# The ten weight buffers of a mixer and MoE layer moved to multiples of 256 bytes in SBUF

## Chip, cores and metric

One Trainium2 chip, one of its cores. The metric is the device time of one execution in microseconds (us), the median of several runs. The profile is one further execution with the hardware profiler on; its times are given from the start of its span, which is the time between the first and the last instruction.

## The reference

One layer on 256 tokens of width 1024, all float32. A layer norm comes first. Then two attentions run side by side from one projection `h @ w_in` (1024 x 5120): a differential attention with 4 heads and a chunk attention with 8. Their outputs go through a projection each, are gated, added, and go through `w_out`; a second norm follows. The mixture of experts takes most of the weights:

```python
logits = (t @ w_router + b_router)                  # 32 experts
top_val, top_idx = lax.top_k(logits, TOP_K)         # the best 4 of them for each token
...
hb = xb @ w_exp_in[e] + b_exp_in[e]                 # 1024 -> 2 x 1024
g = jnp.minimum(hb[:, :D_FF], SWIGLU_LIMIT)
u = jnp.clip(hb[:, D_FF:], -SWIGLU_LIMIT, SWIGLU_LIMIT)
a = g * jax.nn.sigmoid(SWIGLU_ALPHA * g) * (u + 1.0)
return a @ w_exp_out[e] + b_exp_out[e]              # 1024 -> 1024
...
h = layer_norm(DEEPNORM_ALPHA * h + f, ln2_g, ln2_b)
```

Each expert has 8 MiB of `w_exp_in` and 4 MiB of `w_exp_out`, so the 32 of them are 384 MiB that must be read once.

## The kernel before

The first part (up to some 200 us) does the norm, the projection, both attentions, the merge and `w_out`. Weights of this part are split on the chip into two float32r parts, which three matmuls multiply (L169 to L171). After it comes the router, and then a loop over 32 places (`for pos in range(NE)`, L1286). Each place takes one expert: its tokens are gathered with one-hot matmuls (L1094), `gemm1` multiplies them with `w_exp_in` (L1144 for 64 token rows, L1147 for 32), `act` is the SwiGLU, `gemm2` multiplies with `w_exp_out` (L1200), and `scatter` adds the gated result to four PSUM banks (L1214). A last norm and the stores end the kernel.

**Buffers of weights.** All large weights land in buffers of 16,384 bytes in each of the 128 partitions, 2 MiB each. There are ten, in four pools: ring_a has five, ring_b two, ring_d one and ring_c two. The loads of `w_in` (13 parts), the branch weights and `w_out` use ring_a alone. From the experts on, a transfer takes the next buffer of a written order, round and round:

```python
order = (ring_b,) * 2 + (ring_a,) * 3 + (ring_d,) + (ring_a,) * 2 + (ring_c,) * 2
```

Each expert is six transfers: four of `w_exp_in` (`load_in`, L983), each of whose descriptors carries 16 KB of one partition, and two of `w_exp_out` (`load_out`, L995), whose descriptors carry 8 KB (the last of them is cut in two). So 192 buffers are filled, by 193 transfers, and after five experts the 30 places of three rounds begin anew. SP issues them all, in the order of the program; a buffer is free again when the matmuls that read it are done. Rows of `w_in` are 2 KB in the buffer.

**Pools.** A partition's memory is filled from both ends. From the left stand const, ring_a, keep, mid, ring_b and ring_d; from the right late, heads and early, which are closed in turn, and ring_c takes late's place. A tile takes its size rounded up to 32 bytes. By the allocation of the kernel before, in bytes of a partition:

| pool | begins at | behind a multiple of 256 | buffers |
|---|---|---|---|
| ring_a | 31,520 | 32 | 5 |
| ring_b | 147,200 | 0 | 2 |
| ring_d | 179,968 | 0 | 1 |
| ring_c | 196,576 | 224 | 2 |

ring_c ends at 229,344, the end of what the right side begins with.

`sub08` and `nlam`, which the change joins, are one column each: DVE writes sub08 at L351 and nlam in `small_1` (L371), and DVE reads them in `differences` (L560) and `finish_a` (L596).

Of the kernel before, what the change touches and what calls it, by code (L numbers as in the profile page):

```python
# [9 lines left out]
F32 = mybir.dt.float32  # L10
# [10 lines left out]
P = 128  # L21
# [23 lines left out]
def kernel(  # L45
# [19 lines left out]
    const = ctx.enter_context(tc.tile_pool(name="const", bufs=1))  # L65
# [2 lines left out]
    es_late, es_heads, es_early = ExitStack(), ExitStack(), ExitStack()  # L68

    keep = ctx.enter_context(tc.tile_pool(name="keep", bufs=1))  # L70
    late = es_late.enter_context(tc.tile_pool(name="late", bufs=1, side="right"))
    heads = es_heads.enter_context(tc.tile_pool(name="heads", bufs=1, side="right"))
    early = es_early.enter_context(tc.tile_pool(name="early", bufs=1, side="right"))
# [266 lines left out]


    bg = const.tile([P, 16], F32, name="bg")
    sub08 = const.tile([P, 1], F32, name="sub08")
    nlam = const.tile([P, 1], F32, name="nlam")
    g1p = early.tile([P, 2 * KC], F32, name="g1p")
    wrg = const.tile([P, KC, NE], F32, name="wrg", tag="wrg")
    rows = const.tile([P, 2, NE], F32, name="rows")
# [338 lines left out]
    def load_rows(src, rows, name, ring):  # L686

        w = wslot(ring, name).rearrange("p (k c) -> p k c", k=4)
        nc.sync.dma_start(w, src[rows:rows + 512, :].rearrange("(k p) c -> p k c", p=P))
        return w  # L690

    wba = load_rows(w_branch_a[0], 0, "wba", ring_a)
    wbb = load_rows(w_branch_b[0], 0, "wbb", ring_a)
    mid = ctx.enter_context(tc.tile_pool(name="mid", bufs=1))
    ring_b = ctx.enter_context(tc.tile_pool(name="ring_b", bufs=2))
    wo = [load_rows(w_out[0], i * 512, f"wo{i}", ring_a) for i in range(2)]

# [711 lines left out]
```

## Time and profile before

| | |
|---|---|
| runs | 1134.95, 1135.90 and 1136.48 us, median 1135.9 |
| profiled execution | 1135.54 us, of which 1133.8 are its span |
| mean granted TensorE clock | 0.947 of full speed |
| busy share of the span | PE 84%, weight load 37%, DVE 25%, ACT 17%, POOL 4% |
| moved by DMA | 438.58 MB, 387 GB/s on the mean |
| chain of work that ended last | DMA 62%, PE 30%, DVE 2%, ACT 1% |

PE is TensorE's matmuls; its busy time is an average over stages with different limits, and so is the DMA rate. The chain is followed back from the last instruction, at each step to what released it. Where it names a DMA, the piece reaches from the issue of the transfer to its landing.

### The profile page before, as it was taken

The page shows a single profiled execution, that of the slowest core. Times are in us where ns is not written, and L with a number is a line of the kernel's source. Part 1 is how long each engine was busy: PE and PEld are TensorE (multiplying, and loading weights), DVE is VectorE, ACT ScalarE, POOL GpSimd, SP SyncE. Part 2 cuts the span into 40 slices and gives each one's busy share as a digit, 9 for nine tenths or more (in the row PEclk, how much of TensorE's full clock was granted, in tenths as well). Part 3 has the DMA queues.
Part 4 walks back from the last instruction along what each step waited for, and adds up shares of the span by engine and source line. Part 5 has one row for each costly group of instructions (what it writes and reads, how often), then busy time and mean ns, then how long its engine had stood idle before and what let it go on. Part 6 is the DMA issues. An engine that isn't in the chain of part 4 may idle for free.

```text
span 1133.8 us, 14138 instructions
## 1 busy us (share of the span) xinstructions
PE 951.6 (84%) x5771; PEld 424.3 (37%) x5771; DVE 282.8 (25%) x640; ACT 191.4 (17%) x412; POOL 48.2 (4%) x77
## 2 busy tenths in 40 slices
PE   8999999999999877878897968787878787878764
PEld 7999998433333222222232312122222122222211
DVE  7687577421111111111111111111111011011113
ACT  4366653211010000000000000000000000000010
POOL 3201200100010000000000000000000000000001
PEclk9999999999999999999898989899989898999978
DMA  8943568899999999999999999999999999999994
GB/s 289 384 174 136 201 249 351 326 403 426 425 412 426 429 426 428 427 425 429 426 425 425 427 428 426 427 425 428 427 425 426 424 428 427 427 427 427 427 423 182
DMA packets 52442, 438.58 MB, mean 387 GB/s; under 512 B 5070, under 2 KB 5422, under 8 KB 19858
## 3 DMA queue, kind: packets, MB, share of 16 engines
q1 hardware_dynamic: 50818, 433.90, 92.0%
q0 software_dynamic: 1120, 3.05, 0.8%
q8 instruction: 47, 0.77, 0.3%
q10 hardware_dynamic: 432, 0.66, 0.2%
q14 instruction: 25, 0.20, 0.1%
HBM read 436.14 MB, written 1.45 MB: 386 GB/s over the span
## 4 chain that ended last, share of the span: by engine, by line
DMA 62%; PE 30%; DVE 2%; ACT 1%; issue 1%; DVEq 0%; SPq 0%; ACTq 0%
DMA w<-in_w_exp_in_dram 52%; DMA w<-in_w_exp_out_dram 10%; PE gu L1144 7%; PE py L1200 4%; PE gu L1147 3%; PE pT L169 2%; PE pT L170 2%; PE pT L171 2%; PE acc L1214 2%; PE px L1094 1%; PE br L171 1%; PE br L170 1%; PE br L169 1%; PE mo L169 1%; PE mo L171 1%; PE mo L170 1%
## 5 line engine op out<-in xcount | busy, mean ns | idle before, releaser
L1144 PE MATMUL gu<-w,xe 128*64 128x512 f32 x1024 | 238.3, 614 | 55.2 <-DMA w<-in_w_exp_in_dram 55.0
L1147 PE MATMUL gu<-w,xe 128*32 128x512 f32 x1024 | 150.5, 720 | 87.5 <-DMA w<-in_w_exp_in_dram 87.5
L1200 PE MATMUL py<-w,aTe 128*64 128x512 f32 (+1 forms) x1024 | 174.8, 604 | 8.6 <-DMA w<-in_w_exp_out_dram 5.4
L1144 PEld LDWEIGHTS gu<-w,xe 128*64 128x64 f32 x1024 | 74.9, 140 | 209.2 <-issue 147.3
L1172 DVE TENSOR_SCALAR a<-gu 128x512 f32<-128x512 f32 (+1 forms) x32 | 17.9, 558 | 468.1 <-PE gu L1144 249.9
L1173 ACT ACTIVATE sg<-a 128x512 f32<-128x512 f32 (+1 forms) x32 | 16.7, 523 | 524.2 <-DVE a L1172 524.2
L1147 PEld LDWEIGHTS gu<-w,xe 128*32 128x32 f32 x1024 | 31.1, 120 | 186.7 <-DMA w<-in_w_exp_in_dram 132.1
L1200 PEld LDWEIGHTS py<-w,aTe 128*64 128x64 f32 (+1 forms) x1024 | 49.9, 124 | 110.3 <-issue 89.4
L169 PE MATMUL pT<-hT_hi,w 128*128 128x256 f32 x256 | 74.0, 289 | 0.0
L170 PE MATMUL pT<-hT_lo,w 128*128 128x256 f32 x256 | 72.4, 283 | 0.0
L171 PE MATMUL pT<-hT_hi,w 128*128 128x256 f32 x256 | 72.4, 283 | 0.0
L1207 DVE COPY y<-py 128x256 f32<-128x256 f32 x32 | 13.6, 425 | 218.1 <-ACT y L1206 212.9
L1214 PE MATMUL acc<-y,st 64*128 64x512 f32 x248 | 61.6, 615 | 0.0
L164 DVE TENSOR_TENSOR w<-win,w 128x512 fp32r<-128x512 f32 (+1 forms) x70 | 51.2, 757 | 31.6 <-ACT w L163 31.6
L163 ACT CAST w<-win 128x512 fp32r<-128x512 f32 (+1 forms) x74 | 46.2, 654 | 33.4 <-PE pT L170 23.1
L1094 PE MATMUL px<-h,oh 128*32 128x256 f32 (+1 forms) x392 | 49.5, 465 | 0.7 <-ACT xe L1119 0.7
L169 PEld LDWEIGHTS pT<-hT_hi,w 128*128 128x128 f32 x256 | 49.0, 191 | 2.2 <-issue 1.4
L170 PEld LDWEIGHTS pT<-hT_lo,w 128*128 128x128 f32 x256 | 49.1, 192 | 0.0
L171 PEld LDWEIGHTS pT<-hT_hi,w 128*128 128x128 f32 x256 | 49.0, 192 | 0.0
L119 POOL TENSOR_TENSOR ln_r<-ln_ve,nhalf 128x1 f32<-128x1 f32 x6 | 3.4, 560 | 849.0 <-DVE ln_ve L117 848.0
L1206 ACT COPY y<-py 128x256 f32<-128x256 f32 x32 | 11.9, 373 | 156.5 <-PE py L1200 156.5
L1214 PEld LDWEIGHTS acc<-y,st 64*128 64x128 f32 x248 | 21.3, 186 | 33.9 <-issue 19.2
(329 smaller groups left out, 827.6 us busy)
## 6 DMA issues: line engine op xcount, KB each, us to landing
w<-in_w_exp_in_dram SPq DMA_DIRECT2D x128, 2048.0 KB, 39.1
w<-in_w_exp_out_dram SPq DMA_DIRECT2D x63, 2048.0 KB, 39.1
win<-in_w_in_dram SPq DMA_DIRECT2D x9, 2048.0 KB, 17.8
wo<-in_w_out_dram SPq DMA_DIRECT2D x2, 2048.0 KB, 7.8
win<-in_w_in_dram SPq DMA_DIRECT2D x4, 512.0 KB
wba<-in_w_branch_a_dram SPq DMA_DIRECT2D x1, 2048.0 KB
wbb<-in_w_branch_b_dram SPq DMA_DIRECT2D x1, 2048.0 KB
w<-in_w_exp_out_dram SPq DMA_DIRECT2D x2, 1024.0 KB, 38.3
```

The source lines that it names most:

```text
L163: A.copy(hi, part)
L164: (eng[k // step % len(eng)] if isinstance(eng, tuple) else eng).tensor_tensor(lo, part, hi, op=ALU.subtract)
L169: T.matmul(dst, a[0], b[0], start=first, stop=False)
L170: T.matmul(dst, a[0], b[1], start=False, stop=False)
L171: return T.matmul(dst, a[1], b[0], start=False, stop=last)
L1094: T.matmul(px[i * w:(i + 1) * w, :], oh[:, t, :], h1[:, t, i * n:(i + 1) * n], start=(t == 0), stop=(t == NT - 1))
L1144: T.matmul(gu[i][q * w:(q + 1) * w, :], lhsT, rows[:, i, q * c:(q + 1) * c], start=first, stop=last)
L1147: T.matmul(both[q * w:(q + 1) * w], lhsT, rows[:, :, q * c:(q + 1) * c], start=first, stop=last)
L1172: V.tensor_scalar(g, gu[0], SW_LIMIT, None, op0=ALU.min)
L1173: A.activation(sg, g, AF.Sigmoid, scale=SW_ALPHA)
L1200: T.matmul(py[r:r + w, :], lhsT, w2[i][:, q, j, n * 512:(n + 1) * 512], start=(i == 0 and (m == 0 or w < CAP and m < 2)), stop=(i == 1 and ...
L1214: T.matmul(acc[t][n], st[r, t, :], y[r, :], start=False, stop=False)
```

## The change

A pool edge of 56 floats (224 bytes) is put at the right end, ahead of late, heads and early; the two tiles of one column in const become two columns of one tile, which makes const 32 bytes shorter; and a tile of 8 floats (32 bytes) is put at the start of mid. Nothing uses edge and mid_pad. By that the right side moves down by 224 bytes, ring_c to 196,352, which is 767 x 256 and just where ring_d ends; ring_a and keep move down by 32, ring_a to 31,488, which is 123 x 256; ring_b (575 x 256) and ring_d (703 x 256) stay where they are. No instruction is added, taken away or moved.

```diff
@@ -68,6 +68,9 @@
     keep = ctx.enter_context(tc.tile_pool(name="keep", bufs=1))
+
+    edge = ctx.enter_context(tc.tile_pool(name="edge", bufs=1, side="right"))
+    edge.tile([P, 56], F32, name="edge")
     late = es_late.enter_context(tc.tile_pool(name="late", bufs=1, side="right"))
@@ -340,8 +343,8 @@
     bg = const.tile([P, 16], F32, name="bg")
-    sub08 = const.tile([P, 1], F32, name="sub08")
-    nlam = const.tile([P, 1], F32, name="nlam")
+    two_cols = const.tile([P, 2], F32, name="two_cols")
+    sub08, nlam = two_cols[:, 0:1], two_cols[:, 1:2]
     g1p = early.tile([P, 2 * KC], F32, name="g1p")
@@ -692,6 +695,7 @@
     mid = ctx.enter_context(tc.tile_pool(name="mid", bufs=1))
+    mid.tile([P, 8], F32, name="mid_pad")
     ring_b = ctx.enter_context(tc.tile_pool(name="ring_b", bufs=2))
```

## Rows read from the trace of the kernel before

**Rows 1.** The page's slices, 40 of 28.3 us each: the busy share of the 16 DMA engines in tenths, and what they moved.

```profile
DMA  8943568899999999999999999999999999999994
GB/s 289 384 174 136 201 249 351 326 403 426 425 412 426 429 426 428 427 425 429 426 425 425 427 428 426 427 425 428 427 425 426 424 428 427 427 427 427 427 423 182
```

**Rows 2.** The table by stage, for the part with the experts: the stretch, its length, the busy time of PE, weight load, DVE, ACT and POOL (with counts of instructions), the granted clock, the DMA share and GB/s.

```profile
255.00:366.00 111.00, 107.37 (x692) 36.77 (x694) 19.00 (x52) 12.46 (x28) 6.53 (x17) 1.00 1.01 423
366.00:500.00 134.00, 108.01 (x636) 33.94 (x628) 18.62 (x50) 11.58 (x25) 0.00 (x0) 0.95 1.01 427
500.00:700.00 200.00, 159.60 (x864) 50.37 (x864) 26.84 (x69) 14.88 (x32) 0.00 (x0) 0.93 1.01 426
700.00:900.00 200.00, 155.51 (x866) 48.16 (x862) 25.12 (x67) 15.16 (x33) 0.00 (x0) 0.93 1.01 427
900.00:1100.00 200.00, 153.75 (x866) 47.83 (x870) 26.16 (x68) 15.87 (x36) 0.00 (x0) 0.91 1.01 427
```

**Rows 3.** The chain that ended last, in order of time: start, length, what. Between the third and the fourth row stand 15 more pieces of weights of 39 to 41 us, with short pieces of PE between them.

```profile
358.36 7.11 PE py L1200 x32
365.49 32.52 DMA w<-in_w_exp_in_dram
403.10 39.73 DMA w<-in_w_exp_in_dram
...
1068.84 40.95 DMA w<-in_w_exp_in_dram
1109.83 3.22 PE gu L1147 x16
```

**Rows 4.** What SP waited for before its issues from 366 to 1100 us: us in total, times, longest; and the page's issues of expert weights: count, size, median us from issue to landing.

```profile
SPq L983 <- DMA w<-in_w_exp_out_dram: 101.7, 48, 3.5
SPq L995 <- DMA w<-in_w_exp_in_dram: 98.9, 49, 3.4
SPq L983 <- DMA w<-in_w_exp_in_dram: 82.3, 48, 3.1
SPq L983 <- PE py L1200: 44.4, 25, 3.2
...
w<-in_w_exp_in_dram SPq DMA_DIRECT2D x128, 2048.0 KB, 39.1
```

**Rows 5.** The DMA engines' busy share in tenths from 180 to 260 us, 40 slices of 2 us.

```profile
DMA  9999999046999981089999999998799999999999
```

**Rows 6.** SP's issues in order of time: start, time until the last of them is out, line, transfer and count.

```profile
580.19 17.62 SPq L983 DMA_DIRECT2D w<-in_w_exp_in_dram  x4
...
609.71 19.25 SPq L983 DMA_DIRECT2D w<-in_w_exp_in_dram  x4
```

**Rows 7.** Six stretches of 9.8 us, 49.1 us apart, in which the two ring_b places of a round move. Columns as in rows 2.

```profile
614.80:624.60 9.80, 7.33 (x38) 2.34 (x36) 1.23 (x5) 0.37 (x1) 0.00 (x0) 0.83 1.00 430
663.90:673.70 9.80, 8.92 (x56) 3.05 (x56) 2.03 (x5) 1.96 (x4) 0.00 (x0) 1.00 1.03 433
713.00:722.80 9.80, 4.65 (x32) 0.83 (x32) 0.00 (x0) 0.00 (x0) 0.00 (x0) 0.86 0.99 424
762.10:771.90 9.80, 8.53 (x52) 2.38 (x48) 1.26 (x5) 0.37 (x1) 0.00 (x0) 1.00 1.02 435
811.20:821.00 9.80, 8.56 (x52) 3.55 (x54) 3.19 (x5) 1.93 (x4) 0.00 (x0) 1.00 1.00 425
860.30:870.10 9.80, 8.66 (x40) 2.60 (x36) 0.00 (x0) 0.00 (x0) 0.00 (x0) 1.00 1.01 429
```

**Rows 8.** The same for the two ring_c places of a round.

```profile
654.10:663.90 9.80, 6.08 (x32) 1.03 (x32) 0.00 (x0) 0.00 (x0) 0.00 (x0) 0.65 0.99 420
703.20:713.00 9.80, 8.47 (x50) 2.36 (x46) 1.26 (x5) 0.37 (x1) 0.00 (x0) 1.00 1.01 431
752.30:762.10 9.80, 8.54 (x52) 3.53 (x54) 3.19 (x5) 1.91 (x4) 0.00 (x0) 1.00 1.02 422
801.40:811.20 9.80, 8.64 (x38) 2.58 (x34) 0.00 (x0) 0.00 (x0) 0.00 (x0) 0.98 1.01 425
850.50:860.30 9.80, 6.37 (x34) 1.85 (x32) 1.23 (x5) 0.37 (x1) 0.00 (x0) 0.83 1.01 430
899.60:909.40 9.80, 7.41 (x28) 1.86 (x30) 1.60 (x4) 1.00 (x2) 0.00 (x0) 0.65 1.01 419
```

**Rows 9.** All DMA packets that started from 400 to 1000 us.

```profile
DMA packets 22845, 255.98 MB, mean 427 GB/s; under 512 B 1954, under 2 KB 1954, under 8 KB 1954
```

**Rows 10.** Two longer stretches that begin with a ring_b pair (663.9 and 958.5 us, by the rhythm of rows 7) and run past its end. Columns as in rows 2.

```profile
664.00:680.00 16.00, 11.57 (x78) 3.81 (x80) 3.26 (x10) 2.34 (x5) 0.00 (x0) 1.00 1.02 431
961.00:973.00 12.00, 11.21 (x76) 3.50 (x75) 2.03 (x5) 2.34 (x5) 0.00 (x0) 1.00 1.01 432
```

**Rows 11.** A wait from the start to 45 us: us in total, times, longest.

```profile
ACT w L163 <- DMA win<-in_w_in_dram: 4.4, 3, 2.0
```

**Rows 12.** PE's matmuls on the weight buffers in `gemm1` with 64 token rows, from 400 to 1100 us: shortest, median and longest in ns, first and last start, shape.

```profile
L1144 PE MATMUL gu<-w,xe x712: 590/592/1116, 399.8 to 1052.2; 128*64 128x512 f32 x178
```

**Rows 13.** The stretch behind the last landing. Columns as in rows 2.

```profile
1110.00:1115.00 5.00, 5.00 (x25) 1.22 (x22) 1.61 (x4) 0.42 (x1) 0.00 (x0) 0.75 0.76 314
1115.00:1120.00 5.00, 4.02 (x36) 1.48 (x40) 0.42 (x1) 0.37 (x1) 0.00 (x0) 1.00 0.30 123
1120.00:1125.00 5.00, 2.64 (x24) 1.46 (x16) 2.62 (x7) 0.37 (x1) 0.39 (x1) 1.00 0.01 3
```

## The prediction, made before the change was run

> **What bounds the kernel now.** I read the page's slices first [rows 1]: the DMA line stays at 9 and GB/s near 427 from the ninth slice to the last but one. The table by stage [rows 2] says what TensorE does under it. From 255 to 366 us both are full: 107.37 of 111 us of PE, at a DMA share of 1.01. From 366 to 1100 PE is busy 77 to 81% and the DMA engines go on without a pause, at 426 or 427 GB/s. The chain in order of time [rows 3] agrees: PE until 365.49 us, then pieces of weights one behind another, a first of 32.5 us and the others of 39 to 41, the last of which ends at 1109.8; the 24 us behind it are matmuls, the norm and the stores. SP's waits [rows 4] show why nothing else can speed this up: 145 of its issues wait for the landing of an earlier transfer, together 283 us, and the freeing of a buffer by PE is the smaller part. From issue to landing takes 39.1 us, and at 4.9 us for 2 MiB (2.097 MB at 427 GB/s) that is a queue of eight. So each nanosecond per transfer counts from the moment when the queue last ran dry. The slices of 2 us between 180 and 260 [rows 5] put that at about 236 us: the last digits under 9 are those of 232 to 236. To 1109.8 that is **874 us that the DMA engines set**.
>
> **What moves.** By the program's allocation, the two buffers of ring_b and the one of ring_d start on a multiple of 256 bytes already; the five of ring_a start 32 bytes behind one, the two of ring_c 224. So the change is one for seven buffers of ten. The 32 bytes that const loses come back as mid_pad, which leaves ring_b and ring_d where they are. The order of the pieces is fixed: b b a a a d a a c c. Hence the trace of before holds both cases, ten pieces or 49.1 us apart, and I can price the change from it. The 91st and 92nd pieces, both ring_b, are the first two of the group that SP issues from 580.19 us [rows 6]. With 39.1 us to landing they move until about 619 and 624. The ring_c pieces are the last two of the group from 609.71 [rows 6], and move until about 659 and 664. I took the 9.8 us of these two pieces, six rounds of each.
>
> - ring_b, on the boundary [rows 7]: 430, 433, 424, 435, 425, 429, mean **429.3 GB/s**.
> - ring_c, 224 bytes off [rows 8]: 420, 431, 422, 425, 430, 419, mean **424.5 GB/s**.
> - all pieces, 400 to 1000 us [rows 9]: 255.98 MB in 600 us, **426.6 GB/s**. What is left for the five of ring_a, with ring_d taken like ring_b: (4266 - 3 x 429.3 - 2 x 424.5) / 5 = 425.8.
>
> So both shifted kinds move more slowly than the kind on the boundary. Single rows scatter by 4 or 5, since a packet counts where it starts and a round mixes rows of 8 and of 16 KB, which makes each mean uncertain by some 2 GB/s.
>
> What the Trainium skill says of this, on the page "DMA: Bandwidth & Descriptors", section "How a descriptor splits into AXI transactions": a descriptor is cut at multiples of 256 bytes, and one that starts off such a multiple fetches the bytes before its start in vain. The page tells it for the fetching side, and does not say that it holds where a transfer writes. Taken for the writes, 32 bytes are one beat more on 512 (16 KB) or 256 (8 KB), and 224 bytes seven; a place in the order holds 16 KB rows in two rounds of three, so ring_a would pay 0.26%, ring_c 1.8%, the ten together 0.49%, an estimate of 4.3 us by that page. The trace agrees in the order of the kinds and has ring_c at 1.1% under ring_b.
>
> **The sum.** If all ten move at the pace of ring_b, each piece takes 426.6/429.3 of its time, 0.63% less. 874 us x 0.0063 = **5.5 us**. Other terms:
>
> - The stretch from 236 to 365 us is PE's in the chain. I count it in full, since the queue doesn't run dry there [rows 2], and a transfer that ends earlier lets the next begin. If it gave nothing, 744 us would be left, 4.7 us.
> - Lower bound of the pace: nothing at all, if the gap between the two sets is scatter. Upper bound: two longer stretches around ring_b pieces ran at 431 and 432 [rows 10]. Were that the true pace (the 16 engines are not in step, so my windows catch a neighbour's pieces), it would be 1.1% or 9.9 us. I take the six rounds, because the longer stretches were picked for being fast.
> - The loads of w_in go into ring_a too, as rows of 2 KB. Only the first are waited for: ACT waits 4.4 us for them in three waits [rows 11], so one or two hundredths of that are at most 0.1 us. The wait is bounded by other parts of the start; I take nothing.
> - edge and mid_pad have no instruction. sub08 and nlam become columns of one tile; their writers and readers (L351, L371, L560, L596) are all on DVE in the same order, so no engine gets a wait that it didn't have: nothing. The cover is that order alone; without it the price would be one wait for a copy of one column.
> - PE reads the moved weights. Its matmuls on w take 590 ns at the least and 592 in the median in gu of 64 tokens [rows 12]; that name stands for all ten buffers, seven of them off the boundary, and still half of the matmuls lie within those 2 ns. So the start doesn't matter to PE: nothing. Were it to cost a few ns each, PE's idle fifth behind 366 us would hide it.
>
> The profiled execution took 1135.5 us (its span of 1133.8 and 1.7 around it), 0.4 under the median of the three. 1135.5 - 5.5 = **1130.0 us**, a gain of 0.48%.
>
> **The rivals.**
>
> *No change* (0.11). The pace is set at the source, or by the engines' own work per row, and the six rounds differ by luck. For it: the two sets overlap (424 to 435 against 419 to 431), and the mean of each is uncertain by 2. Against it: the residue for ring_a lies on the same side. Also the case in which a fast piece only makes up for the delay of a slow one, so that ten fast ones in a row are no faster than the mix. Time 1135.5. The Trainium skill's page "SBUF — State Buffer" (the section on a bandwidth-pool intuition that's wrong) calls HBM the end-to-end bound, at about 358 GB/s; by that rule this would be the outcome. The trace disagrees with the figure, at 427.
>
> *A larger gain* (0.13). The aligned pace is that of the longer stretches [rows 10], as the skew of the engines dilutes my windows. 1.1% of 874 us: 1125.6.
>
> *Slower* (0.04). TensorE's clock behind the last landing. The 15 us from 1110 hold 11.66 us of PE work [rows 13], which nothing covers; the granted clock there is 0.75, 1.00 and 1.00, so a quarter of 10 us or 2.5 us ran at 1.2 GHz and the rest at 2.4. The landing comes at another moment, and the lower level may fall otherwise. Were the whole tail at 1.2 GHz, the 9.2 us that ran at full clock would take twice that: +9.2, against the 5.5 gained, 1139.2. It decides from 7.8 us on (5.5 and the 2.3 that count as slower), nearly the whole tail. Against it: in the stages behind 366 the mean is 0.91 to 0.95 [rows 2], and the lower level goes with PE's idle time, which a faster DMA shortens. The same thing in small moves the forecast by about 1 us either way.
>
> **How the numbers follow.** The forecast with its scatter (1128.0 to 1132.5) gets 0.72. 0.2% of this kernel is 2.3 us, about what a measurement can tell from no change. Below 1133.2 lie the forecast and the larger gain: faster 0.85, same 0.11, slower 0.04. Range: the no-change and slower cases (0.15) are left out above, and the far end of the larger gain (0.05) below: 1127.0 to 1133.2.
>
> **What would show it.** Right: GB/s of 400 to 1000 us at 429 or more; the ring_c rounds no longer under the ring_b rounds; the pieces of the chain 39.1 us -> 38.9; PE's waits for w shorter by some 5 us in total, PE's busy time unchanged; the last landing at about 1104. The stages before 236 us should stay as they are. Wrong: the same 427 with the sets level, which would mean that their gap was scatter; or a faster DMA with the last landing where it was, which would mean a queue that ran dry between 236 and 365 us; or both right and the time lost behind the last landing.

## The result and the profile after

The changed kernel takes **1129.15 us** (median of 4, 1128.13 to 1129.61) against 1136.03 for the kernel before (median of 4, 1134.95 to 1136.48): a ratio of 0.994 with a 95% interval of 0.9922 to 0.9957, so 6.9 us less. The forecast was 1130.0 in a range of 1127.0 to 1133.2. The profiled executions differ by 6.6 us: 1128.93, with a span of 1127.2, against 1135.5.

The page's slices, answering to [rows 1]:

```profile
DMA  8942568899999999999999999999999999999994
GB/s 280 408 163 116 206 255 359 326 398 429 429 421 429 431 430 429 431 430 427 430 430 428 430 428 429 429 430 430 429 427 430 428 429 429 430 429 430 430 426 185
```

From the tenth slice to the last but two the line stays near 430 instead of 427. The second slice, in which rows of 2 KB of w_in are loaded, went from 384 to 408.

The table by stage, answering to [rows 2], and behind it the twelve short stretches of one pair of pieces each: six of ring_b, answering to [rows 7], then six of ring_c, answering to [rows 8]. The places were found again from the times at which SP issues the pieces. Columns: stretch, length, busy time of PE, weight load, DVE, ACT and POOL, granted clock, DMA share, GB/s.

```profile
255.00:366.00 111.00, 107.35 (x694) 36.81 (x698) 19.29 (x53) 12.48 (x28) 6.50 (x17) 1.00 1.01 427
366.00:500.00 134.00, 108.59 (x636) 33.77 (x630) 19.50 (x54) 11.59 (x25) 0.00 (x0) 0.95 1.01 430
500.00:700.00 200.00, 161.10 (x876) 51.12 (x874) 26.33 (x65) 15.81 (x34) 0.00 (x0) 0.94 1.01 429
700.00:900.00 200.00, 152.31 (x864) 46.04 (x860) 24.39 (x65) 14.26 (x31) 0.00 (x0) 0.94 1.01 429
900.00:1100.00 200.00, 155.54 (x898) 47.87 (x894) 26.17 (x68) 17.53 (x38) 0.00 (x0) 0.93 1.01 429
...
611.40:621.20 9.80, 6.81 (x46) 1.99 (x39) 1.23 (x5) 0.37 (x1) 0.00 (x0) 1.00 1.01 433
660.40:670.20 9.80, 8.62 (x56) 2.89 (x48) 2.03 (x5) 1.96 (x4) 0.00 (x0) 1.00 1.03 434
709.40:719.20 9.80, 5.43 (x32) 1.01 (x32) 0.00 (x0) 0.00 (x0) 0.00 (x0) 0.83 0.99 424
758.40:768.20 9.80, 8.01 (x48) 2.22 (x44) 1.26 (x5) 0.37 (x1) 0.00 (x0) 1.00 1.01 432
807.40:817.20 9.80, 9.20 (x54) 3.68 (x56) 3.19 (x5) 1.92 (x4) 0.00 (x0) 1.00 1.03 435
856.40:866.20 9.80, 7.31 (x32) 2.12 (x32) 0.00 (x0) 0.00 (x0) 0.00 (x0) 1.00 1.00 424
...
650.40:660.20 9.80, 5.24 (x36) 1.06 (x40) 0.00 (x0) 0.00 (x0) 0.00 (x0) 0.83 1.00 428
699.40:709.20 9.80, 8.55 (x52) 2.40 (x48) 1.26 (x5) 0.37 (x1) 0.00 (x0) 1.00 1.01 432
748.40:758.20 9.80, 8.85 (x54) 3.57 (x56) 3.19 (x5) 1.92 (x4) 0.00 (x0) 1.00 1.02 429
797.40:807.20 9.80, 7.31 (x32) 2.12 (x32) 0.00 (x0) 0.00 (x0) 0.00 (x0) 1.00 0.99 423
846.40:856.20 9.80, 7.23 (x51) 2.05 (x40) 1.23 (x5) 0.50 (x2) 0.00 (x0) 1.00 1.00 430
895.40:905.20 9.80, 8.28 (x36) 2.36 (x36) 1.60 (x4) 1.00 (x2) 0.00 (x0) 0.69 1.02 431
```

Every stage with the experts moves 2 to 4 GB/s more, the first one, in which PE is as full as before, as much as the others. The ring_b places hardly moved, from a mean of 429.3 to 430.3; the ring_c places rose from 424.5 to 428.8.

The packets from 400 to 1000 us, answering to [rows 9]; this line is used for every experiment below, because it takes in 600 us of steady transfers and leaves out the start and the tail:

```profile
DMA packets 22912, 257.68 MB, mean 429 GB/s; under 512 B 1958, under 2 KB 1958, under 8 KB 1958
```

257.68 MB in 600 us are 429.5 GB/s, against 426.6. The chain in order of time, answering to the end of [rows 3] (start, length, what):

```profile
1062.78 40.44 DMA w<-in_w_exp_in_dram
1103.27 3.40 PE gu L1151 x16
```

The last landing is at 1103.2 instead of 1109.8, 6.6 us earlier, and 24 us of tail follow in both kernels. So the whole gain of the profiled execution was there when the last piece landed, and the work behind it gave and took nothing. Of the 6.6 us, 874 x (1 - 426.6/429.5) = 5.9 come from the rate.

SP's waits from 366 to 1094 us, answering to [rows 4] (us in total, times, longest):

```profile
SPq L987 <- DMA w<-in_w_exp_out_dram: 96.3, 48, 3.0
SPq L999 <- DMA w<-in_w_exp_in_dram: 91.5, 48, 3.3
SPq L987 <- DMA w<-in_w_exp_in_dram: 75.8, 48, 3.1
SPq L987 <- PE py L1204: 55.5, 29, 3.4
```

The queue still sets the pace: 263.6 us of waits for landings (282.9 before), and the freeing of a buffer by PE comes last a little more often, 29 times instead of 25.

### The profile page after: what moved, and what is told of

Its sections match the earlier page's. It is cut to its first block, busy times and chain, and to the rows that moved or that the text cites. A ratio compares the mean times of both kernels' runs of the same rounds, so it can differ in the third digit from the quotient of the medians.

```text
span 1127.2 us, 14138 instructions
## 1 busy us (share of the span) xinstructions
PE 944.3 (84%) x5771; PEld 419.9 (37%) x5771; DVE 282.8 (25%) x640; ACT 191.4 (17%) x412; POOL 48.1 (4%) x77
## 4 chain that ended last, share of the span: by engine, by line
DMA 59%; PE 34%; DVE 2%; ACT 1%; issue 0%; DVEq 0%; SPq 0%; ACTq 0%
DMA w<-in_w_exp_in_dram 56%; PE gu L1148 7%; PE py L1204 4%; PE gu L1151 4%; DMA w<-in_w_exp_out_dram 3%; PE pT L172 2%; PE acc L1218 2%; PE pT L173 2%; PE pT L174 2%; PE px L1098 2%; PE br L172 1%; PE br L174 1%; PE br L173 1%; PE mo L173 1%; PE mo L172 1%; PE mo L174 1%
## 5 line engine op out<-in xcount | busy, mean ns | idle before, releaser
L1148 PE MATMUL gu<-w,xe 128*64 128x512 f32 x1024 | 233.8, 603 | 53.2 <-DMA w<-in_w_exp_in_dram 53.0
L1148 PEld LDWEIGHTS gu<-w,xe 128*64 128x64 f32 x1024 | 72.0, 138 | 205.4 <-issue 140.3
## 6 DMA issues: line engine op xcount, KB each, us to landing
w<-in_w_exp_in_dram SPq DMA_DIRECT2D x128, 2048.0 KB, 38.8
w<-in_w_exp_out_dram SPq DMA_DIRECT2D x63, 2048.0 KB, 38.9
```

The source lines that it names most:

```text
L1148: T.matmul(gu[i][q * w:(q + 1) * w, :], lhsT, rows[:, i, q * c:(q + 1) * c], start=first, stop=last)
```

## The experiments

Before the first four of them there were four theories of where the gain comes from. **A:** each row that is written to a start off the multiple of 256 costs the same, however far off it is, so the loss goes with the number of buffers that are off. **B:** the price grows with the distance from the multiple. **C:** a coarser rule than the change assumes, with 64 or 128 bytes enough. **D:** the gain doesn't come from the starts, but from something else that the edit moved. Three more were put down after those four runs. **E:** a few buffers off the multiple cost less than their part, as the aligned ones behind them make up for it. Two concern the price itself. **F:** each row of a transfer (one descriptor) has a price of its own beside its bytes. **G:** bytes alone count.

Every kernel below was timed against the kernel before on the same chip. The first four shared a median of 1135.45 us for it, the next four 1135.73, the last two 1135.69. The changed kernel's own time is the 1129.15 of the result and, run again with the last pair, 1128.60; so a difference of half a microsecond between times of two chips says nothing.

### All ten buffers off by the same distance

A tile behind two_cols moves all of the left side, and a shorter edge moves all of the right side by as much, so that all ten buffers lie off the multiple by one distance. Everything else of the change stays. For 32 bytes:

```diff
-    edge.tile([P, 56], F32, name="edge")
+    edge.tile([P, 48], F32, name="edge")
...
     two_cols = const.tile([P, 2], F32, name="two_cols")
+    const.tile([P, 8], F32, name="const_pad")
```

For 64, 128 and 224 bytes const_pad has 16, 32 and 56 floats and edge 40, 24 and none.

> The changed kernel with all ten buffers pushed 32 bytes behind a multiple of 256 (32 more bytes in const, edge 32 bytes smaller). Theory A (any start off the multiple costs each row the same, whatever its distance): seven buffers off cost 6.9 us, so ten cost 6.9 x 10/7 = 9.9 us, 1139.0; 400 to 1000 us at about 425 GB/s. Theory B (the price grows with the distance): 32 bytes is the cheapest case; by the stretches of the kernel before, 425.8 against 429.3 GB/s for ring_a, 0.8% of 874 us or 7.2 us, 1136.4, and the other three distances above it in order. Theory C (a multiple of 64 or of 128 is enough): here as A. Theory D (the gain came from the joined columns or from other tiles that moved, not from the buffers' starts): 1129.2. The Trainium skill's page 'DMA: Bandwidth & Descriptors' (How a descriptor splits into AXI transactions), taken for writes, gives one beat more on 512 or 256, an estimate of 0.26% or 2.3 us: 1131.5.

> All ten buffers 64 bytes behind a multiple of 256. Theory A: 1139.0 as at 32. Theory B: between 32 and 224 bytes, some 1136.9. Theory C, if a multiple of 64 is enough: 1129.2, and GB/s as in the changed kernel (429.5). Theory D: 1129.2. The Trainium skill's page 'DMA: Bandwidth & Descriptors' (How a descriptor splits into AXI transactions), taken for writes: two beats, an estimate of 4.6 us, 1133.7.

> All ten buffers 128 bytes behind a multiple of 256. Theory A: 1139.0. Theory B: some 1137.7. Theory C, if a multiple of 64 or of 128 is enough: 1129.2. Theory D: 1129.2. The Trainium skill's page 'DMA: Bandwidth & Descriptors' (How a descriptor splits into AXI transactions), taken for writes: four beats, an estimate of 9.1 us, 1138.3.

> All ten buffers 224 bytes behind a multiple of 256, the distance that ring_c has in the kernel before. Theory A: 1139.0, the same as at 32. Theory B: the dearest case; by the stretches of the kernel before, 424.5 against 429.3 GB/s, 1.1% of 874 us or 9.8 us, 1139.0, with 32 bytes at 1136.4. Theory C: as A. Theory D: 1129.2. The Trainium skill's page 'DMA: Bandwidth & Descriptors' (How a descriptor splits into AXI transactions), taken for writes: seven beats, an estimate of 15.9 us, 1145.

Measured: 1139.03 us at 32 bytes (ratio to before 1.0031, 1.0019 to 1.0043), 1138.23 at 64 (1.0019, 1.0009 to 1.003), 1138.20 at 128 (1.0023, 1.0013 to 1.0034), 1140.64 at 224 (1.0044, 1.0031 to 1.0058). The packets from 400 to 1000 us, first 32:

```profile
DMA packets 22726, 254.67 MB, mean 424 GB/s; under 512 B 1939, under 2 KB 1939, under 8 KB 1939
```

64:

```profile
DMA packets 22789, 255.20 MB, mean 425 GB/s; under 512 B 1944, under 2 KB 1944, under 8 KB 1944
```

128:

```profile
DMA packets 22801, 255.25 MB, mean 425 GB/s; under 512 B 1943, under 2 KB 1943, under 8 KB 1943
```

224:

```profile
DMA packets 22749, 254.62 MB, mean 424 GB/s; under 512 B 1941, under 2 KB 1941, under 8 KB 1941
```

D falls as far as it is about the joined columns: all four carry them and mid_pad, and are 9.0 to 11.5 us slower than the changed kernel, and slower than the kernel before. The tiles of keep and some of const move along with ring_a in each of these kernels; that the gain is the buffers' and not theirs is seen from the rows that the DMA engines move, below. C falls: with 64 and with 128 bytes most of the loss is there. B falls: 32 and 224 bytes moved the same 254.6 to 254.7 MB, 1.2% under the changed kernel. 64 and 128 are a little cheaper, at 0.95%; why is open. (32 and 224 are odd multiples of 32, 64 and 128 are not; 96, 160 and 192 were not run.) The starts of the changed kernel are all odd multiples of 256, so whether a multiple of 512 gives still more is not shown either. That A's 1139.0 for 32 bytes was met to a tenth is in part luck: it was scaled up from the 6.9 us of the whole change, of which the rate is 5.9, and in proportion to the number of buffers, which the next section takes back.

On the page "DMA: Bandwidth & Descriptors" of the Trainium skill, the section "How a descriptor splits into AXI transactions" counts what a start off the multiple fetches in vain by its distance; carried over to the writes it would have made the ten buffers 2.3 us slower at 32 bytes and 15.9 at 224, an estimate by the same beats as in the prediction. The runs agree that 64 and 128 bytes are not enough, and disagree with a price by distance: 254.67 MB moved at 32 bytes and 254.62 at 224.

The 1.6 us by which 224 is slower than 32 in the medians don't lie where the experts' weights move steadily. The stretch ahead of the experts in the profiles of the two, 32 first:

```profile
198.00:212.00 14.00, 12.81 (x69) 7.06 (x69) 10.07 (x46) 4.50 (x7) 3.63 (x4) 1.00 0.80 312
```

224:

```profile
198.00:212.00 14.00, 13.75 (x63) 8.56 (x64) 9.74 (x48) 4.49 (x7) 3.68 (x4) 0.76 0.81 315
```

TensorE was granted full clock in the one and 0.76 in the other, and the first matmul of an expert began at 208.57 us against 210.96. Half a microsecond of this was there at 196 us already, where the clock was 1.00 in both; at the last landing 1.9 us are left (1113.1 and 1115.0). The kernels off by 128 bytes and, below, with ring_c alone off had 0.76 there as well. So some 2 us can arise ahead of the experts, most of them with the clock; for small differences I go by the packets.

### Two of ten off, and five of ten off

The first is the changed kernel without edge. That puts the two buffers of ring_c back to 224 bytes off:

```diff
-    edge = ctx.enter_context(tc.tile_pool(name="edge", bufs=1, side="right"))
-    edge.tile([P, 56], F32, name="edge")
```

> The changed kernel without edge: ring_c alone is off, by 224 bytes, two buffers of ten. Theory A with the price proportional to the number of buffers that are off (all ten at 32 or 224 bytes measured 1139.0 and 1140.6, some 9.8 to 11 us over the changed kernel): two of ten cost 2.0 us, 1131.2; the ring_c stretches under the ring_b stretches again. Theory E (a lone pair that is off is caught up by the eight that are not, because something between reading and writing holds a reserve): clearly under 2 us, near 1129.2.

The second is the kernel before with edge alone, so that ring_c is on the multiple and the five buffers of ring_a are 32 bytes off:

```diff
+    edge = ctx.enter_context(tc.tile_pool(name="edge", bufs=1, side="right"))
+    edge.tile([P, 56], F32, name="edge")
```

> The kernel before with edge alone: ring_c comes to a multiple of 256, ring_a stays 32 bytes off, five buffers of ten. Theory A, proportional: 4.9 us over the changed kernel, 1134.1, with 427.0 GB/s from 400 to 1000 us. Theory E (reserve): less than 4 us, 1133 or below. With the run in which ring_c alone is off, the two should add up to the 6.9 us of the whole change under A.

Measured: 1129.69 us with ring_c off (0.9944, 0.993 to 0.9957) and 1132.53 with ring_a off (0.9969, 0.9957 to 0.9981). The packets, ring_c off:

```profile
DMA packets 22970, 257.59 MB, mean 429 GB/s; under 512 B 1963, under 2 KB 1963, under 8 KB 1963
```

ring_a off:

```profile
DMA packets 22875, 256.84 MB, mean 428 GB/s; under 512 B 1953, under 2 KB 1953, under 8 KB 1953
```

Measured by the bytes that the changed kernel moved in the same 600 us, the loss is 0.03% with two buffers off, 0.33% with five, 0.66% with seven (the kernel before, [rows 9]) and 1.17% with all ten at 32 bytes. In proportion from the ten it would be 0.23, 0.59 and 0.82. So the loss grows faster than the number: A is right that the distance hardly counts and wrong about a few buffers, and E holds. Two edits that ease one queue don't add up either: seen from the kernel before, aligning the five alone gains 0.63% and the two alone 0.34%, together 0.97%, yet the whole change gained 0.66%. Whichever is made first finds other off buffers beside it, and takes more.

The times point the same way but don't settle it. Measured from 1129.15, undoing the two of ring_c costs 0.5 us and undoing the five of ring_a 3.4 (A: 2.0 and 4.9); measured from the 1128.60 of the changed kernel's second run it is 1.1 and 3.9, and the runs of one of these kernels lie up to 3 us apart.

The packet records of the traces show where the delay lies. From 400 to 1000 us over 99% of the rows of the changed kernel last exactly 611 ns (16 KB) or 309 ns (8 KB). With all ten buffers off by 32 bytes, 95% last more than 1 ns longer; the means are 616.9 ns against 612.0 for 16 KB and 315.6 against 309.9 for 8 KB, so about 5 ns more for a row of either length. In between it depends on the place in the order. Here is the share of rows, in per cent, that last more than 1 ns longer, with the rows sorted by their start and 2 MiB given to each place (the engines are not quite in step, so that a row can stand one place off):

| place | b | b | a | a | a | d | a | a | c | c |
|---|---|---|---|---|---|---|---|---|---|---|
| kernel before | 18 | 0 | 20 | 66 | 78 | 23 | 41 | 90 | 96 | 84 |
| ring_a alone off | 0 | 0 | 5 | 38 | 47 | 18 | 40 | 80 | 23 | 0 |
| ring_c alone off | 9 | 0 | 0 | 0 | 0 | 0 | 0 | 0 | 1 | 15 |
| changed kernel | 0 | 0 | 0 | 0 | 0 | 0 | 0 | 0 | 0 | 0 |

The first buffer that is off behind two or more aligned ones is hardly slower (20, 5 and 1%). The delay builds up from one off buffer to the next, reaches into the aligned one behind (d, and with ring_a alone off the first c), and is gone after one or two of those. So it is a run of off buffers that is paid for, and a pair among aligned ones is not. What holds this reserve, something ahead of the engines or behind them, no run here shows, and none spread the off buffers over the order in another way.

### The price of a row

In the kernel that the change leaves, a piece of w_exp_in moves as 128 rows of 16 KB, and a piece of w_exp_out as 256 of 8 KB. Two kernels change one size each and leave all starts on the multiple. The first halves the rows of w_exp_in, with the transposes of xr in the same order:

```diff
-        src = of_expert(w_exp_in, e).rearrange("(i p k) f -> i p k f", p=P, k=2)
+        src = of_expert(w_exp_in, e).rearrange("(i k p) f -> i p k f", p=P, k=2)
...
-        xv = xr.rearrange("r (i p j) -> r i j p", p=P, j=2)
+        xv = xr.rearrange("r (i j p) -> r i j p", p=P, j=2)
```

> The changed kernel with w_exp_in read as rows of 8 KB in place of 16 KB (the rows of a transfer are dealt to the partitions in another order, and the gathered tokens likewise), all ten buffers on the boundary. Theory F (each descriptor has a price of its own, which an off start adds to): in the trace of the changed kernel a packet of 16 KB takes 611 ns of an engine and one of 8 KB 309, 7 ns more for the same bytes at most and by the spacing of their starts 4.4; 16 rows in place of 8 on each engine make a transfer 35 ns longer, and the 116 of w_exp_in in the stretch 4.1 us: 1133.3. Theory G (only bytes and boundaries count): 1129.2.

Measured: 1133.75 us (0.9977, 0.9966 to 0.9987).

```profile
DMA packets 33220, 256.29 MB, mean 427 GB/s; under 512 B 1957, under 2 KB 1957, under 8 KB 1957
```

G falls and F holds: the same bytes to the same buffers in more rows cost 4.6 us. In the 600 us it is 0.54% fewer bytes, or 3.2 us of transfer time, for 10,309 more rows (33,220 less 1957 small ones, against 22,912 less 1958), 644 on each of the 16 engines: about 5.0 ns a row. All ten buffers off by 32 bytes cost 1.17%, 7.0 us, on 1299 rows of each engine, or 5.4 ns a row. So a start off the multiple costs about what one more row does.

The edit changes more than the number of rows: they are read from DRAM in another order, and from issue to landing a piece took 32.7 us in place of 38.8, with SP waiting for buffers that PE frees and no longer for landings. The engines still set the pace: their busy share is 1.01 in every stage behind 255 us, as before. That it is the number of rows and not their order is not separated by the pace alone, but the packet records speak for it. A row of 8 KB lasts 309.4 ns on the mean here and 309.9 in the changed kernel, where only w_exp_out has such rows, in an order of its own; two of them last 6.8 ns longer than one row of 16 KB.

The second kernel joins the two halves of a row of w_exp_out, for the experts of full width (15 places in the order):

```diff
+    def wide(pos):
+        return width(pos) == CAP and pos != SECOND
...
+        if wide(pos) and not tiles:
+            src = of_expert(w_exp_out, e).rearrange("(i p k) c -> i p k c", p=P, k=4)
+            for i in range(2):
+                w = piece(f"w2_{pos}_{i}")
+                nc.sync.dma_start(w.rearrange("p (k c) -> p k c", k=4), src[i])
...
+        aw = a.rearrange("r (p j) -> r j p", j=4) if base == 0 and wide(pos) else None
```

> The changed kernel with w_exp_out read as rows of 16 KB in place of 8 KB for 15 experts (the places with 64 token rows, except the one whose overflow block reads the same weights in 32 rows); the SwiGLU's result is turned four columns apart in place of two. Theory F: 30 transfers, 29 of them in the stretch, each 35 ns shorter, 1.0 us: 1128.2. Theory G: 1129.2. If the transposes with the wider step slow TensorE, that is covered while it waits for weights, except at the start of the experts, where some tenths of a us could be lost.

> The changed kernel once more, on the chip of the next run, so that the two can be compared: 1129.2, as measured with the prediction. It also gives the zero for ring_c alone off (1129.7) and ring_a alone off (1132.5): with a reserve (theory E) they stay at 0.5 and 3.3 us over it; were it itself 1 us off, they would not.

> The kernel with w_exp_out in rows of 16 KB for 15 experts, beside the changed kernel on one chip. Theory F: 1.0 us under the changed kernel (it measured 1.6 under, on another chip). Theory G: no difference; then the first was scatter of the chips.

Measured: 1127.53 us (0.9931, 0.9917 to 0.9945) beside the narrower rows; then, on one chip, 1127.86 (0.9929, 0.9917 to 0.9941) against 1128.60 for the changed kernel (0.9932, 0.9919 to 0.9945). The packets of that last pair, the changed kernel first:

```profile
DMA packets 22911, 257.65 MB, mean 429 GB/s; under 512 B 1959, under 2 KB 1959, under 8 KB 1959
```

The wide rows:

```profile
DMA packets 20267, 257.92 MB, mean 430 GB/s; under 512 B 1961, under 2 KB 1961, under 8 KB 1961
```

Both lines repeat, within 0.03 MB, what the first profile of the same kernel had (257.68 and, for the wide rows, 257.94), so the 0.1% between them is there and is about 0.9 us of 874. In the 600 us it is 0.63 us for 165 rows fewer on each engine, 3.8 ns a row. The times differ by 0.7 us in the same direction, but their intervals overlap. The wide rows are the fastest version that was run, by an amount that the time alone doesn't settle.

## Why the prediction was right, and where its steps were not

**The size.** 5.5 us were forecast from 429.3 GB/s. The changed kernel ran at 429.5, worth 5.9 us, and its profile began the first expert 0.3 us earlier; the medians differ by 6.9. What is left, 0.7 us, is within the 1.5 us by which the runs of either kernel differ among themselves, and no run here assigns it. The pieces of the chain came to 38.9 us as forecast, and the last landing to 1103.2, where about 1104 was said. Two readings were off without effect: the last digits under 9 in [rows 5] are those of 234 to 238 us, and not of 232 to 236; and the ninth slice of [rows 1] is still at 403 GB/s, so that 427 begins with the tenth.

**The pace of the aligned pieces.** Taking the six ring_b rounds [rows 7] and not the longer stretches [rows 10] was right: 429.3 read, 429.5 come true, and the rows of the two ring_b places were indeed nearly free of delay in the kernel before (18 and 0%). That the two figures agree to 0.2 GB/s is luck: the prediction itself gave each mean 2 GB/s of uncertainty, where the whole gain is 2.9, and its stretches lie some 2 us late (by the starts of their rows the 91st and 92nd pieces move from 612.5 to 622.2 us, not from 614.8 to 624.6). The larger gain at 431 to 432 didn't come.

**The price by ring.** This step read ring_c's rounds [rows 8] as what these two buffers cost, 1.1%; the sum didn't use it. With ring_c alone off the multiple, the whole pace is 0.03% under the aligned one. The "case in which a fast piece only makes up for the delay of a slow one", put under *no change*, exists, without making ten aligned buffers as slow as the mix: it is what hides two off buffers among eight. The rows of ring_c are slow in the kernel before (96 and 84%) because they stand behind two off pieces of ring_a; the same two buffers at the same distance have 1 and 15% when ring_a is aligned. And ring_c's rounds didn't come level with ring_b's, which was to be a sign: 428.8 against 430.3 with every start on the multiple, so that some 1.5 of the 4.8 GB/s between the two sets need not have been the starts'; the prediction's 2 GB/s of uncertainty covers it.

**The early stretch in full.** Right: 255 to 366 us went from 423 to 427 GB/s, PE as full as before, and the last landing moved by 6.6 us, not by the smaller figure without that stretch.

**The loads of w_in.** The effect was mis-sized, its worth was not, and the sign that the stages before 236 us stay as they are didn't hold. Rows of 2 KB are shorter, so a price for each row would be a larger share of them; no run here changes these rows alone. From 28 to 57 us the kernel before has

```profile
28.00:57.00 29.00, 28.51 (x260) 26.68 (x258) 17.27 (x37) 10.82 (x29) 7.89 (x10) 1.00 1.04 384
```

and the changed one

```profile
28.00:57.00 29.00, 28.31 (x262) 26.84 (x262) 18.30 (x38) 10.28 (x26) 7.90 (x10) 1.00 1.05 408
```

That is 6% more, not one or two hundredths. PE is busy 28.3 of 29 us there, a cover that leaves it worth at most the 0.3 us by which the first expert began earlier.

**PE.** Its matmuls on the weights kept their 590 and 592 ns [rows 12]:

```profile
L1148 PE MATMUL gu<-w,xe x704: 590/592/1116, 440.8 to 1046.2; 128*64 128x512 f32 x176
```

The prediction also said that PE's waits for w would be shorter by 5 us and its busy time unchanged. That was wrong: from 200 us on, the waits went from 147.9 us, the sum of

```profile
PE gu L1147 <- DMA w<-in_w_exp_in_dram: 87.5, 38, 4.4
PE gu L1144 <- DMA w<-in_w_exp_in_dram: 55.0, 39, 2.5
...
PE py L1200 <- DMA w<-in_w_exp_out_dram: 5.4, 6, 1.6
```

to 146.6 us, the sum of

```profile
PE gu L1151 <- DMA w<-in_w_exp_in_dram: 89.4, 37, 3.2
PE gu L1148 <- DMA w<-in_w_exp_in_dram: 53.0, 41, 2.5
...
PE py L1204 <- DMA w<-in_w_exp_out_dram: 4.2, 3, 2.0
```

while PE's busy time fell from 951.6 to 944.3. The mean granted clock went from 0.947 to 0.954 between the two profiled executions. The likely account, which no run here isolates, is that matmuls at the higher level are shorter and the waits behind them longer by as much. How much the kernel gained can't be read from it: the four runs of the changed kernel had clocks of 0.943 to 0.954, and the one at 0.943 took 1129.37 us, the one at 0.953 1129.61. The last landing does tell it.

**The rivals.** *No change* is out by the interval. *Slower* didn't occur, with a tail of 24 us in both.

## What to carry to other kernels

Where a queue of large transfers sets the end, lay the buffers it writes at multiples of 256 bytes of a partition: here that took no instruction, only a few bytes of padding, and was worth 0.6% with seven of ten off and 0.8 to 1.0% with all ten off. Then give each descriptor as long a row as the consumer can use, since a row has a price of its own, here about 5 ns. Where a trace holds both cases, slow and fast, side by side in one queue, read from it the pace of the fast ones, and not what each slow one costs by itself: the delay of one piece can come from the pieces ahead of it.

## What was not expected of the hardware

- The distance from the multiple hardly counts: 32 and 224 bytes off cost the same 1.2%, 64 and 128 bytes 0.95%.
- Two buffers of ten off the multiple cost 0.03% of the rate and five 0.33%, where the ten cost 1.17%. So aligning all but a few of the buffers gives nearly all of the gain. The first buffers to be aligned give more than their part: three of the ten (ring_b and ring_d in the kernel before) take the loss from 1.17 to 0.66%.
- A row off the multiple need not be slower: behind aligned buffers all but 1 and 15% of the rows of ring_c's two places stayed within 1 ns of the shortest.
- Rows of 8 and 16 KB still differ: with w_exp_in in rows of 8 KB the queue moved 256.29 MB in 600 us, against 257.68.
